# Value product with weight units taken in pairs and first pieces on two DMA queues, residual load and index-key norm moved

## The chip, the cores and the metric

The kernel runs on one core of a Trainium2 chip. The metric is the device time of one execution in microseconds (us), taken as the median of several runs; less is better. One further execution was profiled, and all rows below come from that one.

## What is computed

One decoder block on a sequence of 256 positions of 1024 channels, in float32. Cut to the parts that this change touches:

```
proj = h @ w_in[i]
u, v, q, k, vv, q_idx, k_idx, w_idx, g_a, g_b = jnp.split(proj, SPLIT_POINTS, axis=-1)
...
k_idx = layer_norm(k_idx, ln_kidx_g[i], ln_kidx_b[i])
b_out = dsa_attention(q, k, vv, q_idx, k_idx, w_idx)
mix = sigmoid(g_a) * (a_out @ w_branch_a[i]) + sigmoid(g_b) * (b_out @ w_branch_b[i])
y = mix @ w_o[i]
h = layer_norm(ALPHA * h + y, ln1_g[i], ln1_b[i])
...                                   # FFN with a causal convolution, second norm
```

`vv` is the value product, the first of the kernel. The indexer scores of `dsa_attention` need the normalised `k_idx`. The residual `h` in `ALPHA * h + y` is the input `x`.

## The kernel before

**Weights.** All weights stream from DRAM once as units of 128 x 2048 float32 (1 MB), in the order of use, through `prefetch` (line 83) and `take`. A unit lands in a raw buffer (pool `rawp`, three buffers) by a DMA issued on SyncE (SP). `split` (line 74) then writes a rounded copy `hi` on ScalarE (ACT, line 77) and the rest `lo = raw - hi` on VectorE (DVE, line 78); both are kept in pools of five. A product is the sum of three: x_hi w_hi, x_lo w_hi, x_hi w_lo. `take()` asks for units up to four ahead of the one in use. A raw buffer is free again when its `lo` is written.

**The start.** Eight warm-up matmuls run on constants (line 121). The input, transposed and cut into eight x blocks of 128 channels (`xt_sb`, 128 KB each), is split into `xh` and `xl`. `load_unit` (line 130) brings unit 0 in four pieces of 256 KB with one x block after each, unit 1 in two, then x blocks 4 to 7 in one load, then unit 2 in two; unit 3 comes whole through `prefetch`.

**The value product** (line 239) has four accumulators of 128 x 512 in PSUM. Units 0 and 1 hold the two column halves for x blocks 0 to 3, units 2 and 3 those for blocks 4 to 7. The loop takes one unit at a time: four x blocks, each three parts for two row tiles, six matmuls of 512 columns a block, 96 in all. Copies to SBUF (line 243) follow each of the last two units. Index queries (`qi`), the small index-key product (`kwb`), queries, keys and gates follow.

**Index keys.** `kidx_norm` (normalisation of the index keys, on PE, DVE and ACT) is hooked into the first half of the first query unit, `kidx_transpose` into the first half of the third; `indexer_head` runs for heads 0 to 3 behind the third query unit and for 4 to 7 behind the fourth.

**The residual.** After the output gates (line 464) the residual `hres` is loaded into slot `ga`, which the gates use until then (line 468, GpSimd's queue, POOL). `o_half(t, hf)` multiplies by `w_o` for row tile t and column half hf, then adds the residual (line 488) and takes statistics (489). `ln1_apply` normalises (lines 415, 416), and `h_transpose` transposes on PE (line 503). The order is o_half(0,0), o_half(0,1), ln1_apply(0), o_half(1,0), h_transpose(0, ...), o_half(1,1).

**What sets the order.** Each engine runs its instructions in the order in which a scheduler at build time has put them, close to the order of the code. SP waits in order, too: a DMA that must wait for a free buffer, or for one of eight completion semaphores that DMAs use in turn (`DMAHW0` to `DMAHW7`), holds back those behind it.

Of the kernel before, what the change touches and what calls it, by code (L numbers as in the profile page):

```python
# [9 lines left out]
F32 = mybir.dt.float32  # L10
# [5 lines left out]
P = 128  # L16
L = 256
D = 1024
# [22 lines left out]
def kernel(  # L41
# [88 lines left out]
    def load_unit(pieces, pre=None):  # L130
        i = state["next"]
        state["next"] += 1
        raw = rawp.tile([P, UN], F32, tag="raw", name=f"raw{i}")
        hi = hip.tile([P, UN], F32R, tag="hi", name=f"hi{i}")
        lo = lop.tile([P, UN], F32R, tag="lo", name=f"lo{i}")
        n = UN // pieces
        for c in range(pieces):
            cs = slice(c * n, (c + 1) * n)
            nc.sync.dma_start(out=raw[:, cs], in_=wst[i][:, cs])
            if pre:  # L140
                pre(c)
                with tc.issue_after(prev.ins) if c else nullcontext():
                    nc.vector.tensor_copy(xh[:, c:c + 1], xt_sb[:, c:c + 1])
                nc.vector.tensor_tensor(out=xl[:, c:c + 1], in0=xt_sb[:, c:c + 1], in1=xh[:, c:c + 1].bitcast(F32),
                                        op=ALU.subtract)
            m = max(1, n // 512)
            for d in range(m):
                ds_ = slice(c * n + d * n // m, c * n + (d + 1) * n // m)
                prev = split(hi[:, ds_], lo[:, ds_], raw[:, ds_])[1]
        units[i] = (hi, lo)  # L150

    load_unit(4, lambda c: load_x(c, c + 1))
    load_unit(2)
    load_x(4, 8)
    split(xh[:, 4:8], xl[:, 4:8], xt_sb[:, 4:8])
    load_unit(2)
# [20 lines left out]
    def fm_chunks(hi, lo, m2, bank, hook=None):  # L177
        wh = hi.rearrange("p (k n) -> p k n", n=256)
        wl = lo.rearrange("p (k n) -> p k n", n=256)
        for c in range(2):  # L180
            cs = slice(c * P, (c + 1) * P)
            fm_tile(bank[:, c], lambda k: wh[:, k, cs], lambda k: wl[:, k, cs], m2, hook if c == 0 else None)

    def fm_unit(name, m2, hook=None):
        hi, lo = take()
        bank = bankA([P, 2, 2, L], name)
        fm_chunks(hi, lo, m2, bank, hook)
        return bank
# [43 lines left out]
    for kh in range(2):  # L232
        for hf in range(2):
            hi, lo = take()
            for k in range(4):
                for n, (a, b) in enumerate(((xh, hi), (xl, hi), (xh, lo))):
                    kk = 4 * kh + k
                    for t in range(2):
                        nc.tensor.matmul(vbanks[2 * t + hf], a[:, kk, t * P:(t + 1) * P], b[:, k * 512:k * 512 + 512],  # L239
                                         start=kk == 0 and n == 0, stop=kk == KC - 1 and n == 2)  # L240
            if kh == 1:
                for t in range(2):
                    nc.scalar.copy(vv[:, t, hf * 512:(hf + 1) * 512], vbanks[2 * t + hf])
# [56 lines left out]

    def causal_fill(dst, fill):
# [155 lines left out]

    m2 = slot("x2", [P, 2, 8, L], F32R, name="m2")
# [8 lines left out]
    hres = slot("ga", [P, 2, D], name="hres")  # L467
    nc.gpsimd.dma_start(out=hres, in_=x.rearrange("(t p) d -> p t d", p=P))
    l1p = slot("k", [P, 2, D], name="l1p")
    ln1_g = load_par(l1p[:, 0], "ln1_g")  # L470
    ln1_b = load_par(l1p[:, 1], "ln1_b")
    cv_sb = const.tile([P, 4, 44], F32, name="cv_sb")
    nc.sync.dma_start(out=cv_sb, in_=cv)
# [256 lines left out]
```

## Time and profile before

| | us |
|---|---|
| median of 3 runs | 462.25 |
| lowest and highest | 462.13 and 463.82 |
| the profiled execution, whole | 462.86 |
| span of its instructions | 461.1 |
| PE busy | 450.6 (98%) |
| DVE busy | 356.7 (77%) |
| ACT busy | 260.8 (57%) |

The span runs from the first instruction of the program to the last. PE's busy time is modelled: a matmul that has to wait in the middle of a stream counts as busy, so starts of neighbouring matmuls say more than busy shares. PEld is the loading of PE's stationary operand, beside the matmuls. An entry in brackets at a row's end is the idle time of the engine before it, and what ended it.

### The profile page before, as it was taken

The page shows a single profiled execution, that of the slowest core. Times are in us where ns is not written, and L with a number is a line of the kernel's source. Part 1 is how long each engine was busy: PE and PEld are TensorE (multiplying, and loading weights), DVE is VectorE, ACT ScalarE, POOL GpSimd, SP SyncE. Part 2 cuts the span into 40 slices and gives each one's busy share as a digit, 9 for nine tenths or more (in the row PEclk, how much of TensorE's full clock was granted, in tenths as well). Part 3 has the DMA queues.
Part 4 walks back from the last instruction along what each step waited for, and adds up shares of the span by engine and source line. Part 5 has one row for each costly group of instructions (what it writes and reads, how often), then busy time and mean ns, then how long its engine had stood idle before and what let it go on. Part 6 is the DMA issues. An engine that isn't in the chain of part 4 may idle for free.

```text
span 461.1 us, 6365 instructions
## 1 busy us (share of the span) xinstructions
PE 450.6 (98%) x2470; PEld 388.3 (84%) x2470; DVE 356.7 (77%) x582; ACT 260.8 (57%) x381; POOL 9.0 (2%) x19
## 2 busy tenths in 40 slices
PE   8999999999999999999999899999999999999993
PEld 5788898888888888888888699888888888888883
DVE  3869869977787559588785769999878778777746
ACT  3678744466656447645454228987656655656500
POOL 0000001020000100001000000000000000000000
PEclk9999999999999999999999999999999999999998
DMA  7979763555433644737746026846755554551002
GB/s 221 388 271 343 266 239 136 183 183 183 182 124 151 224 171 156 248 117 252 298 179 244 31 92 247 302 153 212 273 182 183 183 188 178 207 200 50 1 0 91
DMA packets 14989, 86.83 MB, mean 188 GB/s; under 512 B 1648, under 2 KB 2928, under 8 KB 5744
## 3 DMA queue, kind: packets, MB, share of 16 engines
q1 hardware_dynamic: 13536, 81.98, 49.1%
q0 software_dynamic: 1136, 4.19, 2.7%
q8 instruction: 19, 0.31, 0.3%
q10 hardware_dynamic: 288, 0.26, 0.2%
q14 instruction: 10, 0.08, 0.0%
HBM read 85.39 MB, written 1.05 MB: 187 GB/s over the span
## 4 chain that ended last, share of the span: by engine, by line
PE 78%; issue 8%; DVE 6%; DMA 5%; ACT 1%; SPq 1%; POOL 0%; DVEq 0%; POOLq 0%; ACTq 0%
PE up L173 16%; PE up L175 8%; PE g L173 6%; PE dn L109 4%; PE dn L110 4%; PE dn L111 4%; PE g L175 3%; PE k L173 3%; PE u L173 3%; DVE lo L78 3%; PE vv L239 3%; PE wb L173 2%; PE u L175 2%; PE k L175 2%; PE v L109 2%
## 5 line engine op out<-in xcount | busy, mean ns | idle before, releaser
L78 DVE TENSOR_TENSOR lo<-raw,hi 128x1024 fp32r<-128x1024 f32 (+1 forms) x158 | 180.0, 1169 | 51.6 <-ACT hi L77 50.7
L77 ACT CAST hi<-raw 128x1024 fp32r<-128x1024 f32 (+1 forms) x158 | 152.7, 1006 | 94.5 <-PE up L173 16.8
L173 PE MATMUL up<-h,hi 128*128 128x512 f32 x320 | 80.3, 392 | 0.0
L173 PEld LDWEIGHTS up<-h,hi 128*128 128x128 f32 x320 | 57.9, 189 | 10.6
L175 PEld LDWEIGHTS up<-h,lo 128*128 128x128 f32 x320 | 43.7, 190 | 3.1
L175 PE MATMUL up<-h,lo 128*128 128x256 f32 x320 | 44.6, 282 | 0.0
L531 ACT ACTIVATE y<-upf,cv_sb 128x256 f32<-128x256 f32 x40 | 21.9, 594 | 20.3 <-DVE upf L194 20.3
L173 PE MATMUL g<-x,hi 128*128 128x512 f32 x128 | 32.9, 399 | 0.0
L173 PEld LDWEIGHTS g<-x,hi 128*128 128x128 f32 x128 | 23.0, 189 | 4.3 <-DVE kT L194 0.2
L532 DVE SCALAR_TENSOR_TENSOR y<-upf,cv_sb,y 128x255 f32<-128x255 f32 x40 | 18.7, 479 | 9.4 <-ACT y L531 9.4
L239 PE MATMUL vv<-hi,x 128*128 128x512 f32 x64 | 19.3, 424 | 0.7 <-ACT hi L77 0.6
L534 DVE SCALAR_TENSOR_TENSOR y<-upf,cv_sb,y 128x254 f32<-128x254 f32 x40 | 18.8, 480 | 1.0
L175 PEld LDWEIGHTS g<-x,lo 128*128 128x128 f32 x128 | 17.4, 190 | 1.3
L175 PE MATMUL g<-x,lo 128*128 128x256 f32 x128 | 17.8, 282 | 0.0
L239 PEld LDWEIGHTS vv<-hi,x 128*128 128x128 f32 x64 | 12.8, 205 | 5.1 <-ACT hi L77 1.5
L173 PE MATMUL wb<-b,hi 128*128 128x512 f32 x64 | 16.3, 396 | 0.0
L173 PE MATMUL k<-x,hi 128*128 128x512 f32 x64 | 16.2, 395 | 0.0
L173 PE MATMUL q<-x,hi 128*128 128x512 f32 x64 | 16.2, 394 | 0.0
L173 PE MATMUL u<-x,hi 128*128 128x512 f32 x64 | 16.1, 393 | 0.0
L173 PE MATMUL wa<-a,hi 128*128 128x512 f32 x64 | 16.0, 392 | 0.0
L194 DVE TENSOR_TENSOR upf<-up,upf 128x512 f32<-128x512 f32 x20 | 13.7, 683 | 0.5 <-ACT upf L193 0.5
L173 PEld LDWEIGHTS k<-x,hi 128*128 128x128 f32 x64 | 11.5, 189 | 2.2 <-DVE kT L194 0.2
(222 smaller groups left out, 819.9 us busy)
## 6 DMA issues: line engine op xcount, KB each, us to landing
raw<-in_wst_dram SPq DMA_DIRECT2D x72, 1024.0 KB, 4.8
raw<-in_wst_dram SPq DMA_DIRECT2D x4, 512.0 KB, 8.7
raw<-in_wst_dram SPq DMA_DIRECT2D x4, 256.0 KB, 4.9
a2a<-in_par_dram POOLq DMA_DIRECT2D x2, 512.0 KB, 5.9
l1p<-in_par_dram POOLq DMA_DIRECT2D x2, 512.0 KB, 6.8
hres<-in_x_dram POOLq DMA_DIRECT2D x1, 1024.0 KB, 7.3
xt_sb<-in_xt_dram SPq DMA_DIRECT2D x4, 128.0 KB, 4.8
xt_sb<-in_xt_dram SPq DMA_DIRECT2D x1, 512.0 KB, 8.9
```

What stands on the lines that cost most here:

```text
L77: a = nc.scalar.copy(hi, src)
L78: return a, nc.vector.tensor_tensor(out=lo, in0=src, in1=hi.bitcast(F32), op=ALU.subtract)
L109: nc.tensor.matmul(ps, ah, bh, start=start, stop=False)
L110: nc.tensor.matmul(ps, ah, bl, start=False, stop=False)
L111: nc.tensor.matmul(ps, al, bh, start=False, stop=stop)
L173: nc.tensor.matmul(ps, wh(k), m2[:, :, k, :], start=k == 0, stop=False)
L175: nc.tensor.matmul(ps[:, 0, :], wl(k), m2[:, 0, k, :], start=False, stop=k == KC - 1)
L194: nc.vector.tensor_tensor(out=dst, in0=bank[:, :, 0, :], in1=dst, op=ALU.add)
L239: nc.tensor.matmul(vbanks[2 * t + hf], a[:, kk, t * P:(t + 1) * P], b[:, k * 512:k * 512 + 512], start=kk == 0 and n == 0, stop=kk == KC - ...
L531: nc.scalar.activation(y[:, c, :], b[:, c, :], AF.Identity, scale=cv_sb[:, 2, ch:ch + 1], bias=cv_sb[:, 3, ch:ch + 1])
L532: nc.vector.scalar_tensor_tensor(y[:, c, 1:], b[:, c, :L - 1], cv_sb[:, 1, ch:ch + 1], y[:, c, 1:], op0=ALU.mult, op1=ALU.add)
L534: nc.vector.scalar_tensor_tensor(y[:, c, 2:], b[:, c, :L - 2], cv_sb[:, 0, ch:ch + 1], y[:, c, 2:], op0=ALU.mult, op1=ALU.add)
```

## The change

The first two units, and then units 2 and 3, are opened as a pair (`open_pair`). In each of x blocks 0 to 3 both units of the pair get two DMA pieces of 128 x 256 (128 KB). For the first block one piece of each unit is issued on ACT's queue, the others on SP's. For the first block half of unit 0's `hi` is made on DVE instead of ACT. x blocks 4 to 7 come in two loads with halves of units 2 and 3. The matmul loop takes each x block through both units. The four copies of the result come at the end. `kidx_norm` is hooked into the second half of its query unit, heads 0 to 3 into the first half of the fourth. The residual goes to slot `q`, which held the gated values `vn` (read last by `spatial`), and its load is written ahead of the `wa` product; the first FFN tile takes slot `ga` in return.

```diff
+    def split_x(a, b, after=None):
+        with tc.issue_after(after.ins) if after else nullcontext():
+            c = nc.vector.tensor_copy(xh[:, a:b], xt_sb[:, a:b])
+        return c, nc.vector.tensor_tensor(out=xl[:, a:b], in0=xt_sb[:, a:b], in1=xh[:, a:b].bitcast(F32), op=ALU.subtract)
...
+    first_two = open_pair()
+    u0, u1 = first_two
+    load_w(u0, 0, 256)
+    load_w(u0, 256, 512, nc.scalar)
+    load_x(0, 1)
+    load_w(u1, 0, 256, nc.scalar)
+    load_w(u1, 256, 512)
+    prev = None
+    for c in range(4):
+        cs = slice(c * 512, (c + 1) * 512)
+        if c:
+            load_x(c, c + 1)
+            for u in first_two:
+                load_w(u, c * 512, c * 512 + 256)
+                load_w(u, c * 512 + 256, c * 512 + 512)
+        cast, xs = split_x(c, c + 1, prev)
+        if c:
+            for u in first_two:
+                nc.scalar.copy(u[2][:, cs], u[1][:, cs])
+            after = xs
+        else:
+            nc.scalar.copy(u0[2][:, 0:256], u0[1][:, 0:256])
+            with tc.issue_after(cast.ins):
+                w = nc.vector.tensor_copy(u0[2][:, 256:512], u0[1][:, 256:512])
...
+            nc.scalar.copy(u1[2][:, cs], u1[1][:, cs])
+            after = xs
+        with tc.issue_after(after.ins):
+            for u in first_two:
+                prev = low(u, c * 512, c * 512 + 512)
+    pair = open_pair()
+    for c in range(2):
+        load_x(4 + 2 * c, 6 + 2 * c)
+        for u in pair:
+            load_w(u, c * 1024, c * 1024 + 1024)
...
     for kh in range(2):
-        for hf in range(2):
-            hi, lo = take()
-            for k in range(4):
-                for n, (a, b) in enumerate(((xh, hi), (xl, hi), (xh, lo))):
-                    kk = 4 * kh + k
+        pair = [take() for _ in range(2)]
+        for k in range(4):
+            kk = 4 * kh + k
+            for n, (a, part) in enumerate(((xh, 0), (xl, 0), (xh, 1))):
+                for hf in range(2):
                     for t in range(2):
-                        nc.tensor.matmul(vbanks[2 * t + hf], a[:, kk, t * P:(t + 1) * P], b[:, k * 512:k * 512 + 512],
+                        nc.tensor.matmul(vbanks[2 * hf + t], a[:, kk, t * P:(t + 1) * P], pair[hf][part][:, k * 512:k * 512 + 512],
                                          start=kk == 0 and n == 0, stop=kk == KC - 1 and n == 2)
...
     for u in range(4):
-        b = fm_unit(f"q{u}", x2, {0: kidx_norm, 2: kidx_transpose}.get(u))
+        b = fm_unit(f"q{u}", x2, *{0: (kidx_norm, 1), 2: (kidx_transpose, 0), 3: (lambda: heads(0, 4), 0)}.get(u, ()))
         fold(b, qT[:, 2 * u:2 * u + 2, :])
-        if u > 1:
-            for h in range(4 * u - 8, 4 * u - 4):
-                indexer_head(h)
+    heads(4, 8)
...
+    hres = slot("q", [P, 2, D], name="hres")
+    nc.gpsimd.dma_start(out=hres, in_=x.rearrange("(t p) d -> p t d", p=P))
...
-    hres = slot("ga", [P, 2, D], name="hres")
-    nc.gpsimd.dma_start(out=hres, in_=x.rearrange("(t p) d -> p t d", p=P))
...
-    f_slots = ["q", ("fa", 0), ("fa", 1), ("fx", 0), ("fx", 1), "k"]
+    f_slots = ["ga", ("fa", 0), ("fa", 1), ("fx", 0), ("fx", 1), "k"]
```

The order of instructions as built shows three places. First SP's DMAs where unit 3 (`raw3`) is loaded, the kernel before, with what each waits for (`DVE` is the release of a raw buffer):

```order
L139 DMA raw1_120<-in_wst_dram 128x1024 [waits DMAHW1_49]
L128 DMA xt_sb_91<-in_xt_dram 128x1024 [waits DMAHW2_49]
L139 DMA raw2_136<-in_wst_dram 128x1024 [waits DMAHW3_49]
L139 DMA raw2_136<-in_wst_dram 128x1024 [waits DMAHW4_49]
L90 DMA raw3_163<-in_wst_dram 128x2048 [waits DMAHW6_49,DMAHW5_49,DVE_49]
```

The same place on SP in the changed kernel:

```order
L148 DMA raw1_96<-in_wst_dram 128x256 [waits DMAHW3_49]
L128 DMA xt_sb_91<-in_xt_dram 128x512 [waits DMAHW4_49]
L148 DMA raw2_144<-in_wst_dram 128x1024 [waits DMAHW5_49]
L148 DMA raw3_147<-in_wst_dram 128x1024 [waits DMAHW1_49,DMAHW6_49,DMAHW0_49,DVE_49]
L128 DMA xt_sb_91<-in_xt_dram 128x512 [waits DMAHW7_49]
L148 DMA raw2_144<-in_wst_dram 128x1024
L148 DMA raw3_147<-in_wst_dram 128x1024
L90 DMA raw4_190<-in_wst_dram 128x2048 [waits DMAHW3_49,DMAHW2_49,DVE_49]
```

The first half of unit 3, which waits for a free raw buffer, now stands ahead of x blocks 6 and 7 and of the second halves of units 2 and 3. Second, the first rows on DVE, before (`x2` holds `xh` and `xl`):

```order
L143 CAST x2_92<-xt_sb_91 128x256 [waits DMAHW1_49]
L144 TENSOR_TENSOR x2_92<-xt_sb_91,x2_92 128x256 [waits DVE_49]
L78 TENSOR_TENSOR lo0_95<-raw0_93,hi0_94 128x512 [waits DMAHW0_49,Activation_49]
L143 CAST x2_92<-xt_sb_91 128x256 [waits DMAHW3_49]
L78 TENSOR_TENSOR lo0_95<-raw0_93,hi0_94 128x512 [waits DMAHW2_49,Activation_49]
```

And after:

```order
L132 CAST x2_92<-xt_sb_91 128x256 [waits DMAHW3_49]
L177 CAST hi0_94<-raw0_93 128x256 [waits DMAHW0_49]
L133 TENSOR_TENSOR x2_92<-xt_sb_91,x2_92 128x256 [waits DVE_49]
L152 TENSOR_TENSOR lo0_95<-raw0_93,hi0_94 128x512 [waits DMAHW1_49,DVE_49,Activation_49]
L152 TENSOR_TENSOR lo1_98<-raw1_96,hi1_97 128x512 [waits DMAHW4_49,DMAHW2_49,Activation_49]
L132 CAST x2_92<-xt_sb_91 128x256 [waits DMAHW5_49]
```

A cast of half the first weight piece has moved to DVE, behind the cast of the x block. Third, on POOL, one piece of the difference:

```order
 L115 DMA a2a<-in_par_dram 128x1024 x2
+L500 DMA hres<-in_x_dram 128x2x1024
 L115 DMA ln_g<-in_par_dram 128x1024
 L115 DMA ln_b<-in_par_dram 128x1024
 L115 DMA l1p<-in_par_dram 128x1024 x2
-L468 DMA hres<-in_x_dram 128x2x1024
```

The residual's load has moved ahead of four parameter loads.

## Rows read from the trace of the kernel before

**Rows 1.** The page, part 1: busy us, share of the span, instructions.

```profile
span 461.1 us, 6365 instructions
...
PE 450.6 (98%) x2470; PEld 388.3 (84%) x2470; DVE 356.7 (77%) x582; ACT 260.8 (57%) x381; POOL 9.0 (2%) x19
```

**Rows 2.** Waits of PE: engine line waited for: us in total, times, longest.

```profile
PE hT L503 <- DVE hres L416: 1.5, 1, 1.5
...
PE kT2ps L284 <- DVE a2a L279: 0.2, 1, 0.2
```

**Rows 3.** Timeline of PE, start: start us, us, engine line op out<-in, count [idle before].

```profile
0.85 3.57 PE L121 MATMUL wps<-const-bfloat16-1.0 128*128 128x512 bf16 x8 [0.85 <-PEq L719]
...
5.00 2.04 PE L239 MATMUL vv<-hi,x 128*128 128x512 f32 x4 [0.58 <-ACT hi L77]
...
14.70 1.07 PE L239 MATMUL vv<-hi,x 128*128 128x512 f32 x4
...
28.30 1.07 PE L239 MATMUL vv<-hi,x 128*128 128x512 f32 x4
...
29.66 1.98 PE L173 MATMUL qi<-x,hi 128*128 128x512 f32 x8
```

**Rows 4.** Windows of line 239 alone: PE busy (matmuls), PEld, clock, DMA share, GB/s.

```profile
5.00:9.40 4.40, 4.40 (x10) 3.44 (x11) 1.00 0.90 213
```

**Rows 5.** Timeline of SP's DMA issues, start.

```profile
0.81 0.37 SPq L139 DMA_DIRECT2D raw<-in_wst_dram  x1
...
4.07 0.43 SPq L128 DMA_DIRECT2D xt_sb<-in_xt_dram  x1
...
11.93 0.33 SPq L90 DMA_DIRECT2D raw<-in_wst_dram  x1
```

**Rows 6.** Timeline of ACT and DVE, start.

```profile
4.27 0.62 ACT L77 CAST hi<-raw 128x512 fp32r<-128x512 f32 x1 [2.19 <-DMA raw<-in_wst_dram]
...
4.56 0.29 DVE L143 CAST x<-xt_sb 128x256 fp32r<-128x256 f32 x1 [4.56 <-DMA xt_sb<-in_xt_dram]
...
5.23 0.68 DVE L78 TENSOR_TENSOR lo<-raw,hi 128x512 fp32r<-128x512 f32 x1
...
11.02 0.29 DVE L143 CAST x<-xt_sb 128x256 fp32r<-128x256 f32 x1 [1.01 <-DMA xt_sb<-in_xt_dram]
```

**Rows 7.** Windows: PE, PEld, DVE, ACT, POOL busy, clock, DMA share, GB/s.

```profile
5.00:9.40 4.40, 4.40 (x10) 3.44 (x11) 2.95 (x7) 1.24 (x2) 0.00 (x0) 1.00 0.90 213
...
13.00:19.00 6.00, 6.00 (x28) 4.94 (x27) 5.57 (x9) 4.89 (x8) 0.00 (x0) 1.00 1.04 419
```

**Rows 8.** DMA issues by tile: count, KB each, median us to landing.

```profile
xt_sb<-in_xt_dram SPq DMA_DIRECT2D x4, 128.0 KB, 4.8
...
wk_sb<-in_wk_dram SPq DMA_DIRECT2D x1, 288.0 KB, 3.3
```

**Rows 9.** Timeline of POOL, DVE and PE where the residual is added and transposed.

```profile
249.17 0.70 POOL L468 DMA_DIRECT2D hres<-in_x_dram  x1 [32.61 <-DVE gb L464]
...
254.76 0.39 PE L109 MATMUL o<-hi,m 128*128 128x512 f32 x1
...
256.55 0.69 DVE L488 SCALAR_TENSOR_TENSOR hres<-hres,o 128x512 f32<-128x512 f32 x1 [6.28 <-DMA hres<-in_x_dram]
...
257.89 0.67 DVE L488 SCALAR_TENSOR_TENSOR hres<-hres,o 128x512 f32<-128x512 f32 x1
...
259.98 0.39 PE L111 MATMUL o<-hi,m 128*128 128x512 f32 x1
...
261.89 1.32 PE L503 MATMUL hT<-ident,hres 128*128 128x128 f32 x8 [1.53 <-DVE hres L416]
```

**Rows 10.** Timeline of POOL behind the last spatial product.

```profile
210.56 0.53 POOL L115 DMA_DIRECT2D ln_g<-in_par_dram  x1 [56.79 <-PE sp L433]
```

**Rows 11.** Timeline of PE at the second key transpose.

```profile
57.60 0.33 PE L284 MATMUL kT2ps<-ident,a2a 128*128 128x128 f32 x1 [0.15 <-DVE a2a L279]
```

**Rows 12.** Timeline of DVE, a pair of weight subtractions beside the index-key chain.

```profile
47.67 2.35 DVE L78 TENSOR_TENSOR lo<-raw,hi 128x1024 fp32r<-128x1024 f32 x2
```

More of the change, by code (lines that the diff above doesn't have):

```diff
@@ L128, in load_x @@
         nc.sync.dma_start(out=xt_sb[:, a:b], in_=xt[:, a:b])
[L130 to L156, printed above, removed]
+    def split_x(a, b, after=None):
+        with tc.issue_after(after.ins) if after else nullcontext():
+            c = nc.vector.tensor_copy(xh[:, a:b], xt_sb[:, a:b])
+        return c, nc.vector.tensor_tensor(out=xl[:, a:b], in0=xt_sb[:, a:b], in1=xh[:, a:b].bitcast(F32), op=ALU.subtract)
+    def open_pair():
+        pair = []
+        for i in (state["next"], state["next"] + 1):
+            raw = rawp.tile([P, UN], F32, tag="raw", name=f"raw{i}")
+            hi = hip.tile([P, UN], F32R, tag="hi", name=f"hi{i}")
+            lo = lop.tile([P, UN], F32R, tag="lo", name=f"lo{i}")
+            units[i] = (hi, lo)
+            pair.append((i, raw, hi, lo))
+        state["next"] += 2
+        return pair
@@ new lines, in load_w, with low @@
+    def load_w(unit, a, b, eng=None):
+        i, raw, _, _ = unit
+        (eng or nc.sync).dma_start(out=raw[:, a:b], in_=wst[i][:, a:b])
+    def low(unit, a, b):
+        _, raw, hi, lo = unit
+        return nc.vector.tensor_tensor(out=lo[:, a:b], in0=raw[:, a:b], in1=hi[:, a:b].bitcast(F32), op=ALU.subtract)
+    first_two = open_pair()
[5 more added lines that the diff above has]
+    load_w(u1, 256, 512)
@@ new lines @@
+    prev = None
[15 more added lines that the diff above has]
+                w = nc.vector.tensor_copy(u0[2][:, 256:512], u0[1][:, 256:512])
+            tc.add_manual_dep(xs.ins, w.ins.name, mybir.DependencyInfo(mybir.DependencyClass.NoSync, mybir.DependencyReason.DATA), reason="order")
+            nc.scalar.copy(u1[2][:, cs], u1[1][:, cs])
[3 more added lines that the diff above has]
+                prev = low(u, c * 512, c * 512 + 512)
@@ new lines @@
+    pair = open_pair()
[3 more added lines that the diff above has]
+            load_w(u, c * 1024, c * 1024 + 1024)
+        _, xs = split_x(4 + 2 * c, 6 + 2 * c, prev)
+        for d in range(2):
+            for u in pair:
+                ds_ = slice(c * 1024 + d * 512, c * 1024 + d * 512 + 512)
+                nc.scalar.copy(u[2][:, ds_], u[1][:, ds_])
+                with tc.issue_after(xs.ins):
+                    prev = low(u, ds_.start, ds_.stop)
@@ L299, in indexer_head, with heads @@
                                                op0=ALU.mult, op1=ALU.add)
+    def heads(a, b):
+        for h in range(a, b):
+            indexer_head(h)
     def causal_fill(dst, fill):
@@ L456 @@
             spatial(u + 2)
+    hres = slot("q", [P, 2, D], name="hres")
+    nc.gpsimd.dma_start(out=hres, in_=x.rearrange("(t p) d -> p t d", p=P))
+    l1p = slot("k", [P, 2, D], name="l1p")
+    ln1_g = load_par(l1p[:, 0], "ln1_g")
+    ln1_b = load_par(l1p[:, 1], "ln1_b")
+    cv_sb = const.tile([P, 4, 44], F32, name="cv_sb")
+    nc.sync.dma_start(out=cv_sb, in_=cv)
     m2 = slot("x2", [P, 2, 8, L], F32R, name="m2")
@@ L465 @@
         split(mh[:, us, :], ml[:, us, :], gb[:, us, :], 0.5)
-    hres = slot("ga", [P, 2, D], name="hres")
-    nc.gpsimd.dma_start(out=hres, in_=x.rearrange("(t p) d -> p t d", p=P))
[L469 to L473, printed above, removed]
     ous = [take(0) for _ in range(4)]
```

14 lines of the change are left out of this document (7 added, 7 removed).

## Prediction

> **What bounds the kernel now.** I read the busy shares first, then who waits for whom on TensorE (PE), then the timelines of the two places that those waits name, and last the DMA rates of the first 20 us. The span is 461.1 us and PE is busy in 98% of it [rows 1], so time can only come from the few places where PE waits or runs slowly. The waits are few: 1.5 us at the transposes of the normalised residual, and 0.2 us at the transpose of the index keys [rows 2]. A third place hides in the busy time: the value product at the start, whose matmuls last longer because they stretch over waits or run at the lower clock. Ten of its matmuls of 512 columns take 4.40 us, 0.44 each [rows 4], the pace of the 1.2 GHz level, as did the eight warm-up matmuls in 3.57 us; from 14.70 to 28.30, ten rounds of six take 13.60 us, 0.227 each [rows 3], the pace of the 2.4 GHz level. (The clock column prints 1.00 in both; the spacing tells the level.) The stage ends when the next product starts, at 29.66 [rows 3]. With the ten slow ones done at 9.40, the other 86 need 86 x 0.227 = 19.5 us and would end at 28.9. So 0.76 us went to waits for data, between 9.40 and 14.70. That is all that a better supply can give once PE runs.
>
> **Part 1, the residual load.** Before, the 1 MB load of the residual stands last on POOL, behind the release of its slot by the last gate sum. It is issued at 249.17, and the first operation that needs it starts at 256.55, after 6.28 us of idle VectorE (DVE) [rows 9]. From the second of those operations (257.89) to the first transpose (261.89) is a chain of 4.00 us: statistics, root, two passes. PE had finished the third output product's last matmul, begun at 259.98, and could have started the transposes 0.227 later, at 260.21. It starts them at 261.89: 1.68 us lost. After, the load takes the slot of the gated values, free once the spatial products have read them. The POOL load that waits for exactly that PE work today goes out at 210.56 [rows 10]; so the residual lands some 30 us before its use. The chain then starts when the second output product ends, about 254.9 (the third starts at 254.76 [rows 9]), and ends at 258.9, 1.3 us before PE asks. I take the whole 1.68. What pays: POOL spends 0.70 us on the issue, with four parameter loads behind it that are used tens of us later; 1 MB of traffic moves from 249 to 211, into a stretch where PE waits for nothing [rows 2] and weights are taken four units ahead. Both at nothing; if the cover failed, 1 MB at the 419 GB/s of large pieces [rows 7] is 2.5 us, against four units of 24 matmuls or their like, 5.4 us each. The swap of the slot for the first FFN tile costs nothing, as both slots are free by 249.
>
> **Part 2, the value product in pairs.** The work stays 96 matmuls and 5 MB. What changes is what PE needs when. Before, one unit goes through four x blocks, six matmuls a block; now two units share a block, twelve matmuls, so a block of 640 KB is asked for every 12 x 0.227 = 2.72 us instead of 384 KB every 1.36. Four terms:
>
> *Start.* Before, the first matmul (5.00) follows the cast of the first x block on DVE (4.56, 0.29 long [rows 6]) by 0.15; the weights' cast on ScalarE (ACT) is done by then. Now DVE does two casts of that size in a row, since half of the first weight piece is cast there: 4.56 + 0.29 + 0.29 + 0.15 = 5.29. This supposes that x lands when it does today: it is the second issue on SP as before. The row for what stands beside it is the rate of the first stage, 213 GB/s between 5.0 and 9.4 [rows 7]: one more 128 KB piece ahead of x (the second unit's, from ACT) is 0.6 us, so up to 5.9; and x could land up to 0.3 earlier, since the piece ahead of it on SP is halved. I take 5.29. The Trainium skill (DMA: Bandwidth & Descriptors, "Issuing engines are not separate DMA queues") says that DMAs issued from several engines share the same DMA engines, and that a second issuer saves only the time of issuing. By it the second unit's piece delays x as if it stood on SP, the start is 5.9, and the forecast would be 460.5.
>
> *Slow stretch.* I keep the rise of the clock at 9.40. From 5.29 that is 9.3 matmuls, and 86.7 are left: 19.65 us, end at 29.05 without waits. Against 29.66 that gains 0.61; from a start at 5.00 it would be 0.77, from 5.9 it is 0.3 (a later start costs half its length, since it is paid in slow matmuls).
>
> *Supply of the first four blocks.* These are 20 pieces of 128 KB, 18 of them on SP. SP issues one every 0.466 us (eight issues from 0.81 to 4.07 [rows 5]), so the last goes out at 0.81 + 17 x 0.466 = 8.7 and lands 4.8 later, by the row of the 128 KB pieces [rows 8]: 13.5. Block 3 begins at 9.40 + 26.7 x 0.227 = 15.45 and wants that piece, cast in 0.62, some 0.5 later: 1.8 us in hand. The slow end: the fourth x block of today, issued at 4.07, landed at 11.02 [rows 5, 6] with 1.57 MB ahead of it, 174 GB/s from 2.0 on; at that pace the 2.62 MB end at 17.1, and PE waits 1.8 us.
>
> *The fourth unit.* There are three raw buffers. The first half of the fourth unit can be issued only when the first unit is split to the end, and the order of SP shows that wait, with the rest of the x blocks and five weight issues behind it. Before, this wait ended at 11.93 [rows 5], and PE came to that unit at 24.2. Now PE wants it right at block 4: 15.45 + 2.72 + 3 x 0.227 = 18.85. The first unit's last piece lands at 12.6, cast 0.62, subtracted 0.68 [rows 6]: issue at 13.9, landing 4.8 later, cast 0.62: 19.3, 0.5 late. With the 3.3 us of the 288 KB load [rows 8] it is 17.8, in time. I take 0.25. At the slow end of the supply it is 2.3 late, on top of the 1.8.
>
> Sum of part 2: 0.61 - 0.25 = 0.36 us gained; bounds +0.77 and 0.61 - 4.1 = -3.5. I choose near the upper end, because the pieces of 4 KB rows and more run at 419 GB/s [rows 7] and the slow pace ends with the first small pieces. The four copies of the result now come together behind the last matmul instead of two and two; their banks are wanted again over 10 us later: nothing.
>
> **Part 3, index keys and heads.** The same instructions move. PE waits for the second key transpose at 57.60, 0.15 us [rows 11]. In DVE's new order the subtraction that stood ahead of the last key additions (half of a pair that takes 2.35 [rows 12]) gives way to a shorter fold, but the whole chain of normalisation hangs on ACT and DVE, and PE now comes earlier by what part 2 gains. Ends: the wait and its refill gone, +0.3; one pair of subtractions late, -2.35. The total work ahead of it is the same, so I take 0. Four heads move into the last query product: same matmuls, no wait there before, nothing.
>
> **Sum.** The profiled execution took 462.86: the 461.1 of the span and 1.76 around it. Less 1.68 + 0.36 + 0 = 2.04 gives 460.8. The median of the runs lies 0.61 under the profiled one, so 462.25 - 2.04 = 460.2.
>
> **Rivals.** *Supply clears it all:* x lands a little earlier, no wait at the fourth unit, the key wait goes: 1.68 + 0.77 + 0.3 = 2.75, 459.5. For it: only 0.5 us is missing at the fourth unit by a pessimistic landing time. Against: the two casts in a row on DVE.
>
> *The clock rises later.* Today it rises after PE ran from 5.00 to 9.40 without a break, behind a break of 0.58 [rows 3, 4]. A later start, or a gap in the first two blocks while the second unit's pieces land, can move the rise. Each us costs 0.5 us (0.44 against 0.227 a matmul). The Trainium skill (TensorE: Matmul & The Clock Gate, Part 1) says that the throttled state is the default and that activity releases it; the two paces in the rows agree. A rise 2 us later takes 1.0: 461.2. Against: twelve slow matmuls are 5.3 us of work on the first block alone, so the next block has time to land.
>
> *Slower: the small pieces.* If 1 KB rows keep the 174 GB/s through all 2.62 MB, block 3 and the fourth unit wait 4.1 us in all, and the time is 462.25 - 1.68 + 3.5 = 464.1. It passes the old time from a loss of 1.7 us in part 2, that is, from 2.3 us of waits: where the early pieces average under some 197 GB/s, so that the last lands at 15.3 and the fourth unit is 2.3 late. For it: 213 GB/s between 5.0 and 9.4 [rows 7], with rows of 1 and 2 KB. Against: the early rate is no worse for having more issues if they stay ahead.
>
> **How the numbers follow.** Forecast 460.2 with its neighbours (459.8 to 460.8) 0.50; supply clears it 0.24; late clock (460.8 to 461.8) 0.18; small pieces 0.08. The range 459.1 to 461.8 leaves out the small pieces and the ends of the others. A measurement of this kernel tells about 0.5% from no change: under 459.94 or over 464.56. Faster by that: nearly all of the second case and about a third of the first, 0.40. Slower by that: half of the last, 0.04. Within: 0.56.
>
> **What would show it.** Part 1 is right if VectorE no longer idles for the residual and the first transposes follow the third product without idle time; wrong if PE still waits there for the second pass. Part 2 is right if the first product of the next stage starts at 29.2 to 29.4, the first value matmul at about 5.3, and PE shows at most a short wait where the fourth unit comes in; wrong if the start is at 5.8 or later, or if the ten or so slow matmuls become fifteen. Part 3 is right if the waits at the key transposes stay under 0.5 us. The forecast falls if a new wait of over 1 us stands in the first 60 us, or if PE waits anywhere from 205 to 250.

## The result and the profile after

The changed kernel takes 467.99 us (median of four runs, 466.96 to 469.0), the kernel before beside it on the same chip 463.03. The ratio is 1.011, with a 95% interval of 1.008 to 1.0139: slower by 5 us, where 2 us faster was forecast. The profiled execution took 466.96, with a span of 465.2 against the 461.1 of [rows 1], so the profile shows 4.1 us of the loss; it is the shortest of the four runs.

The waits of PE first (engine, line, what was waited for: us in total, times, longest):

```profile
PE kwp L305 <- DVE a2a L299: 2.0, 1, 2.0
PE vv L278 <- ACT hi L172: 1.7, 2, 0.8
PE vv L278 <- DVE hi L177: 1.6, 1, 1.6
PE vv L278 <- ACT hi L193: 1.4, 1, 1.4
```

Against [rows 2], the wait of 1.5 us at the residual's transposes (`hT`) is gone, and 5.1 us of waits stand in the value product and at the index keys' first transposes (`kwp`; the 1.6 at the start replaces the 0.58 of [rows 3]). The timeline of PE shows where they are:

```profile
5.72 2.08 PE L278 MATMUL vv<-hi,x 128*128 128x512 f32 x8 [1.61 <-DVE hi L177]
...
12.73 1.66 PE L278 MATMUL vv<-hi,x 128*128 128x512 f32 x6 [0.85 <-ACT hi L172]
...
16.13 2.35 PE L278 MATMUL vv<-hi,x 128*128 128x512 f32 x8 [0.81 <-ACT hi L172]
...
21.45 1.43 PE L278 MATMUL vv<-hi,x 128*128 128x512 f32 x5 [1.38 <-ACT hi L193]
...
32.16 1.98 PE L212 MATMUL qi<-x,hi 128*128 128x512 f32 x8
...
53.63 0.32 PE L305 MATMUL kwp<-ident,a2a 72*128 72x72 f32 x2 [2.02 <-DVE a2a L299]
...
54.07 2.91 PE L212 MATMUL q<-x,hi 128*128 128x512 f32 x8
56.78 1.78 PE L214 MATMUL q<-x,lo 128*128 128x256 f32 x8
58.40 1.99 PE L212 MATMUL q<-x,hi 128*128 128x512 f32 x8
60.23 1.12 PE L214 MATMUL q<-x,lo 128*128 128x256 f32 x8
61.18 1.55 PE L212 MATMUL q<-x,hi 128*128 128x512 f32 x6
...
76.29 2.00 PE L212 MATMUL k<-x,hi 128*128 128x512 f32 x8
```

Follow the starts of the stages. The index queries (`qi`) begin at 32.16 instead of 29.66 [rows 3]: 2.50 us late. The first key unit begins at 76.29; in the trace before it began so:

```profile
70.45 2.00 PE L173 MATMUL k<-x,hi 128*128 128x512 f32 x8
```

That is 5.84 late, so 3.34 more went between the two. Of these, 2.02 are the wait at `kwp`. About 1.55 are the 16 matmuls behind it: from 54.07 to 58.40 they take 4.33 us, and the next 16, from 58.40 to 61.18, 2.78. The windows there (us, PE busy, PEld, DVE, ACT, POOL, granted clock, DMA share, GB/s) tell why:

```profile
53.60:54.80 1.20, 1.17 (x8) 1.07 (x9) 1.20 (x2) 0.53 (x2) 0.00 (x0) 1.00 0.35 75
54.80:58.30 3.50, 3.50 (x14) 3.02 (x13) 3.32 (x8) 3.17 (x4) 0.00 (x0) 0.51 1.02 389
58.30:62.00 3.70, 3.70 (x22) 3.25 (x22) 2.47 (x10) 2.17 (x6) 0.00 (x0) 1.00 0.64 217
```

The granted clock is 0.51 in the middle stretch, the 1.2 GHz level, and 1.00 on both sides; PE had stood idle for 2.02 us until 53.63, and the fall came some 1.2 us behind that.

The supply of weights is behind this, as the experiments below show. SP's issues in the value stage, and the first issue behind them:

```profile
10.17 1.30 SPq L128 DMA_DIRECT2D xt_sb<-in_xt_dram  x1
11.52 5.64 SPq L148 DMA_DIRECT2D raw<-in_wst_dram  x2
17.21 0.43 SPq L128 DMA_DIRECT2D xt_sb<-in_xt_dram  x1
```

The two issues in the middle are the first halves of units 2 and 3. An issue takes some 0.45, so SP stood for about 4.7 us ahead of the second, until 16.7: unit 3 had to wait for unit 0's raw buffer, and everything else waited behind it. The buffer came free so late because unit 0's last piece came late. ACT could start on it only at 15.46, and DVE's subtraction, the first of the two below, ended near 16.8:

```profile
15.46 1.31 ACT L172 CAST hi<-raw 128x512 fp32r<-128x512 f32 x2 [2.78 <-DMA raw<-in_wst_dram]
16.11 1.38 DVE L152 TENSOR_TENSOR lo<-raw,hi 128x512 fp32r<-128x512 f32 x2 [0.67 <-ACT hi L172]
```

The same windows of both traces (columns as above), first after, then before:

```profile
10.00:12.00 2.00, 1.88 (x9) 1.23 (x7) 0.64 (x1) 0.00 (x0) 0.00 (x0) 1.00 0.72 114
12.00:14.00 2.00, 1.27 (x6) 1.05 (x7) 0.69 (x1) 0.62 (x1) 0.00 (x0) 1.00 0.95 288
14.00:16.00 2.00, 1.32 (x6) 0.75 (x4) 0.72 (x2) 0.54 (x1) 0.00 (x0) 1.00 0.85 281
16.00:18.00 2.00, 1.87 (x7) 1.30 (x8) 1.85 (x4) 0.70 (x2) 0.00 (x0) 1.00 0.13 43
```

```profile
10.00:12.00 2.00, 1.97 (x9) 1.11 (x7) 0.99 (x4) 0.23 (x1) 0.00 (x0) 1.00 1.03 414
12.00:14.00 2.00, 1.86 (x8) 1.42 (x8) 1.32 (x3) 1.60 (x3) 0.00 (x0) 1.00 1.01 414
14.00:16.00 2.00, 2.00 (x10) 1.67 (x9) 1.57 (x4) 1.74 (x3) 0.00 (x0) 1.00 1.04 428
16.00:18.00 2.00, 2.00 (x10) 1.65 (x10) 2.00 (x3) 1.77 (x4) 0.00 (x0) 1.00 1.01 410
```

In these 8 us 1.45 MB came instead of 3.33. The missing 1.9 MB are 4.6 us at 410 GB/s. There are two holes, one from 10 to 12 (114 GB/s while the DMA engines are busy 0.72 of the time) and one from 16 to 18 (43 GB/s, the engines busy 0.13 of it). In the first hole only SP's queue moved bytes (244 packets, 0.23 MB), so no other stream took the engines' time.

How this reaches the index keys stands in the timelines of ACT and DVE:

```profile
45.88 2.00 ACT L77 CAST hi<-raw 128x1024 fp32r<-128x1024 f32 x2 [1.79 <-DMA raw<-in_wst_dram]
```

```profile
50.79 2.36 DVE L78 TENSOR_TENSOR lo<-raw,hi 128x1024 fp32r<-128x1024 f32 x2
53.07 0.41 DVE L299 TENSOR_TENSOR a2a<-kwb,a2a 72x256 f32<-72x256 f32 x1
```

A unit's weights land late: ACT casts them at 45.88, after 1.79 us without work, and all that stands behind on ACT and DVE is late with them. On DVE a pair of subtractions, that of the next unit, stands ahead of the index keys' sum (line 299), and PE waits for that sum. Before, the sum ran at 47.33, ahead of such a pair [rows 12]:

```profile
47.33 0.42 DVE L260 TENSOR_TENSOR a2a<-kwb,a2a 72x256 f32<-72x256 f32 x1
```

The last stage went as the prediction said. The transposes start behind the last product without idle time:

```profile
265.72 0.39 PE L111 MATMUL o<-hi,m 128*128 128x512 f32 x1
265.95 1.03 PE L544 MATMUL hT<-ident,hres 128*128 128x128 f32 x8
266.74 0.48 PE L109 MATMUL o<-hi,m 128*128 128x512 f32 x1
```

### The profile page after: what moved, and what is told of

It reads as the page before. It is cut to its first block, busy times and chain, and to the rows that moved or that the text cites. A ratio compares the mean times of both kernels' runs of the same rounds, so it can differ in the third digit from the quotient of the medians.

```text
span 465.2 us, 6391 instructions
## 1 busy us (share of the span) xinstructions
PE 450.1 (97%) x2470; PEld 387.9 (83%) x2470; DVE 358.7 (77%) x586; ACT 260.3 (56%) x380; POOL 8.1 (2%) x19
## 3 DMA queue, kind: packets, MB, share of 16 engines
HBM read 85.39 MB, written 1.05 MB: 186 GB/s over the span
## 4 chain that ended last, share of the span: by engine, by line
PE 87%; DMA 7%; DVE 3%; SPq 1%; ACT 1%; issue 0%; DVEq 0%; ACTq 0%
PE up L212 16%; PE up L214 8%; DMA raw<-in_wst_dram 7%; PE g L212 6%; PE dn L110 4%; PE dn L109 4%; PE dn L111 4%; PE g L214 3%; PE k L212 3%; PE wb L212 3%; PE wa L212 3%; PE u L212 3%; PE q L212 3%; PE wa L214 2%; PE wb L214 2%; PE u L214 2%
## 5 line engine op out<-in xcount | busy, mean ns | idle before, releaser
L78 DVE TENSOR_TENSOR lo<-raw,hi 128x1024 fp32r<-128x1024 f32 x142 | 169.8, 1224 | 50.6 <-ACT hi L77 49.6
L77 ACT CAST hi<-raw 128x1024 fp32r<-128x1024 f32 x142 | 143.5, 1049 | 90.2 <-PE up L212 17.2
L278 PE MATMUL vv<-hi,x 128*128 128x512 f32 x64 | 17.2, 401 | 4.7 <-ACT hi L172 1.7
L278 PEld LDWEIGHTS vv<-hi,x 128*128 128x128 f32 x64 | 11.5, 188 | 9.6 <-ACT hi L172 2.9
L212 PE MATMUL q<-x,hi 128*128 128x512 f32 x64 | 17.2, 411 | 0.0
L152 DVE TENSOR_TENSOR lo<-raw,hi 128x512 fp32r<-128x512 f32 x16 | 10.6, 689 | 6.5 <-ACT hi L193 3.4
```

The source lines that it names most:

```text
L77: a = nc.scalar.copy(hi, src)
L78: return a, nc.vector.tensor_tensor(out=lo, in0=src, in1=hi.bitcast(F32), op=ALU.subtract)
L212: nc.tensor.matmul(ps, wh(k), m2[:, :, k, :], start=k == 0, stop=False)
L278: nc.tensor.matmul(vbanks[2 * hf + t], a[:, kk, t * P:(t + 1) * P], pair[hf][part][:, k * 512:k * 512 + 512], start=kk == 0 and n == 0, st ...
```

## The experiments

Each is a kernel of its own, timed beside the kernel before (its median lay between 462.55 and 463.03 in every group). I write "own place" for an own SBUF slot of the fourth unit's raw weights.

### Each part alone

**e1_residual**: the kernel before with the residual's load moved, and with it the parameter loads written behind it, as in the change.

```diff
-    hres = slot("ga", [P, 2, D], name="hres")          # behind the wa product
+    hres = slot("q", [P, 2, D], name="hres")           # ahead of it
...
-    f_slots = ["q", ("fa", 0), ...
+    f_slots = ["ga", ("fa", 0), ...
```

> The kernel before with the residual's slot and load moved alone. Theory (three separate effects): this part gains what the two traces show between the gate product and the first FFN product, about 1.9 us, so 461.1 where the kernel before has 463.0, a ratio of 0.996; no idle time of TensorE ahead of the transposes of the normalised residual. Rival (the gain shows only because the kernel after comes late there): within 0.3 us of the kernel before.

Measured: 461.06, ratio 0.9952 (0.9933 to 0.997), span 459.2. PE no longer waits at `hT`, and the product behind the transposes begins at 261.03 instead of 262.96, 1.93 us earlier (first this run, then the kernel before):

```profile
261.03 0.48 PE L109 MATMUL o<-hi,m 128*128 128x512 f32 x1
```

```profile
262.96 0.48 PE L109 MATMUL o<-hi,m 128*128 128x512 f32 x1
```

Part 1 stands.

**e2_keys**: the kernel before with the hooks of the index keys and heads moved.

```diff
-        b = fm_unit(f"q{u}", x2, {0: kidx_norm, 2: kidx_transpose}.get(u))
+        b = fm_unit(f"q{u}", x2, *{0: (kidx_norm, 1), 2: (kidx_transpose, 0), 3: (lambda: heads(0, 4), 0)}.get(u, ()))
...
+    heads(4, 8)
```

> The kernel before with the index-key norm and the heads moved alone. Theory (the 2.0 us wait ahead of the index-key transposes and the lower clock behind it come from the late supply of weights out of the value stage): within 0.5 us of the kernel before, 463.0, and no wait at those transposes. Rival (they come from the moved norm itself): 2.5 to 4 us slower, 466 to 467, with a wait of about 2 us at the first index-key transposes.

Measured: 462.75, ratio 0.999 (0.9971 to 1.0008). By itself part 3 costs nothing: the wait at `kwp` in the changed kernel is not the fault of the hooks.

**e3_pairs**: the kernel before with the value product in pairs and its new loads.

```diff
-    load_unit(4, lambda c: load_x(c, c + 1))
+    first_two = open_pair()
...
-        for hf in range(2):
-            hi, lo = take()
+        pair = [take() for _ in range(2)]
```

> The kernel before with the value product in pairs and its small first pieces alone, norm and residual as before. Theory (the value stage costs 2.5 us itself and its late supply another 3.5 at the index keys): 468.5 to 470, the first query-index product starting near 32.2, and a wait of 2 us or a little more at the first index-key transposes. Rival (the wait comes from the moved norm): 465 to 466, and no wait at the index keys.

Measured: 469.57 (468.41 to 473.08), ratio 1.014 (1.0087 to 1.0193). The whole loss is in part 2, and it shows the same two places: the index queries start at 30.96 (32.2 was expected), and PE waits for the index keys although their hooks are the old ones:

```profile
53.76 0.32 PE L305 MATMUL kwp<-ident,a2a 72*128 72x72 f32 x2 [3.36 <-DVE a2a L299]
```

Here PE came to that point 1.2 us earlier than in the changed kernel and left it 0.13 later. So an earlier arrival of PE did not help: what it waits for came no earlier.

**e4_fold_first**: in the changed kernel, the loading and splitting of one unit put behind the index keys' sum, so that its subtractions no longer stand ahead of that sum on DVE.

```diff
-        b = fold(fm_unit(f"qi{u}", x2), name=f"qif{u}")
+        b = fold(fm_unit(f"qi{u}", x2, ahead=AHEAD - u), name=f"qif{u}")
...
-    nc.vector.tensor_tensor(out=kwT[0:72, :], in0=kwb[:, 0], in1=kwT[0:72, :], op=ALU.add)
+    kwf = nc.vector.tensor_tensor(out=kwT[0:72, :], in0=kwb[:, 0], in1=kwT[0:72, :], op=ALU.add)
+    with tc.issue_after(kwf.ins):
+        prefetch(cur["i"] + AHEAD - 1)
```

> The kernel after with one weight unit's loading and splitting put behind the fold of the index keys on VectorE, so that this fold no longer stands behind a pair of weight subtractions. Theory (TensorE's 2.0 us wait there is this one pair in VectorE's order, and the drop of the clock behind it follows from the wait): wait under 0.3 us, no lower clock there, 3.4 us faster than the kernel after, about 464.5. Rival (the fold is late in any case, since its inputs are late): wait over 1 us and a time within 1 us of the kernel after, 467 to 468.

Measured: 467.11 (464.71 to 468.07). Only 0.9 us came back, which is within the spread of the runs. The wait stayed (2.72 us in this profile), and a second one appeared at the next transposes:

```profile
52.94 0.32 PE L307 MATMUL kwp<-ident,a2a 72*128 72x72 f32 x2 [2.72 <-DVE a2a L299]
...
63.13 0.33 PE L325 MATMUL kT2ps<-ident,a2a 128*128 128x128 f32 x1 [1.45 <-DVE a2a L320]
```

On ACT the unit ahead of that one waits 3.36 us for its raw weights, and ACT's copy of the key sum stands behind it:

```profile
47.45 2.00 ACT L77 CAST hi<-raw 128x1024 fp32r<-128x1024 f32 x2 [3.36 <-DMA raw<-in_wst_dram]
...
50.63 0.37 ACT L298 COPY a2a<-kwb 72x256 f32<-72x256 f32 x1
```

My theory of the order fell: with the weights late, the sum waited in the new order too.

### The supply: buffer or small pieces

**e5_256kb**, on the changed kernel:

```diff
-                load_w(u, c * 512, c * 512 + 256)
-                load_w(u, c * 512 + 256, c * 512 + 512)
+                load_w(u, c * 512, c * 512 + 512)
```

and likewise in the first block, all on SP.

> The changed kernel with the first two units in pieces of 256 KB instead of 128 KB, all on SP's queue; the pairs, the order of the matmuls and the rest stay. Buffer theory (the fourth unit waits for a raw buffer that the pair gives back late, and SP stands still with all weights behind it): SP is still held until about 16 to 17 us, the wait for the index keys stays, 466.5 to 468.5. Rival (the 128 KB pieces move too slowly): the first four blocks land earlier, the waits of 0.85 and 0.81 us go and the weights behind come earlier too, 463.5 to 465.5.

**e6_own_raw**, on the changed kernel:

```diff
+            if i == 3:
+                raw = slot("ga", [P, UN], name="raw3")
+            else:
+                raw = rawp.tile([P, UN], F32, tag="raw", name=f"raw{i}")
-            raw = rawp.tile([P, UN], F32, tag="raw", name=f"raw{i}")
```

> The changed kernel with a place of its own in SBUF for the raw weights of the fourth unit (the slot of the first gate tile, free then), so that its load waits for no buffer. Buffer theory: SP runs on at 11.5 us, the rate between 16 and 18 us is above 200 GB/s instead of 43, the 1.38 us before the fourth unit go, and with the supply 3 to 5 us earlier the wait for the index keys (2.0 us) and the half clock behind it (1.7 us) shrink: 462.5 to 465.5. Rival (small pieces): the pieces of blocks 2 and 3 land as late as now, and at best the 1.38 us before the fourth unit go, which the wait for the index keys then swallows: 466.5 to 468.

**e8_both**: both edits.

> Both edits: pieces of 256 KB on one queue and an own place for the fourth unit's raw weights. If buffer hold and small pieces each cost something, this is the fastest of the three, 461.0 to 463.0, near the old kernel less the 1.9 us of the residual. If it lies with the own place alone, within 0.5 us, only the buffer counts; if with the 256 KB alone, only the pieces. If it stays above 465, neither is the cause, and the order of the matmuls itself is (two units must be split before the second block).

Measured: 465.67 (462.44 to 466.77) with large pieces, 463.13 (0.998 to 1.0015 of before) with the own place, 460.92 (0.9946 to 0.9976) with both. From 467.99 that is 2.3, 4.9 and 7.1: the two causes add up within the spread of the runs, and the buffer is the larger. With both gone the kernel is as fast as with part 1 alone (461.06); a gain from the pairs doesn't show. The large pieces alone came out between the two cases set for them (463.5 to 465.5, and 466.5 to 468.5), as both count; in that profile SP was still held, but only until 13.4. The windows show the two holes close one by one; first the own place, then both edits:

```profile
10.00:12.00 2.00, 1.99 (x9) 1.31 (x7) 1.01 (x2) 0.44 (x1) 0.00 (x0) 1.00 0.88 124
...
16.00:18.00 2.00, 2.00 (x6) 1.56 (x5) 1.86 (x5) 0.76 (x3) 0.00 (x0) 0.51 0.90 288
```

```profile
10.00:12.00 2.00, 2.00 (x9) 1.61 (x9) 1.97 (x6) 1.26 (x3) 0.00 (x0) 1.00 1.05 380
...
16.00:18.00 2.00, 2.00 (x11) 1.65 (x10) 2.00 (x5) 1.15 (x2) 0.00 (x0) 1.00 1.03 381
```

With the own place the wait at `kwp` falls to 0.26 us, with both it is gone:

```profile
51.23 0.32 PE L308 MATMUL kwp<-ident,a2a 72*128 72x72 f32 x2 [0.26 <-DVE a2a L302]
```

With the own place the hooks, the pairs and the order on DVE up to the key sum are as in the changed kernel, and the weights come earlier. With both edits one thing more differs: the scheduler has put the key sum ahead of the two pairs of subtractions (it runs at 43.34), so that run by itself doesn't part supply and order; e6_own_raw does.

### Which small pieces

**e13_first_only**, own place, small pieces over two queues in the first block alone:

```diff
-                load_w(u, c * 512, c * 512 + 256)
-                load_w(u, c * 512 + 256, c * 512 + 512)
+                load_w(u, c * 512, c * 512 + 512)
```

> The kernel with the fourth unit's own raw place (463.13), with 128 KB pieces over two queues in the first x block only and 256 KB pieces in blocks 1 to 3. If the two queues and small pieces of the first block cost the early supply, it stays at 462.5 to 463.5; if the twelve small pieces of blocks 1 to 3 do, it goes to the 460.9 of the kernel with 256 KB throughout, 460.5 to 461.5.

**e14_one_queue**, own place, all small pieces on SP:

```diff
-    load_w(u0, 256, 512, nc.scalar)
+    load_w(u0, 256, 512)
...
-    load_w(u1, 0, 256, nc.scalar)
+    load_w(u1, 0, 256)
```

> The kernel with the fourth unit's own raw place (463.13), with all its 128 KB pieces on SP's queue and none on ACT's. If the second queue slows the early packets of the first, it is faster, 461 to 462.5; if only the number of pieces counts, it stays at 462.7 to 463.7, the first value matmul up to 0.9 us later for the two issues more on SP ahead of x.

**e12_2kb_rows**, own place, as many 128 KB pieces in blocks 1 to 3, but of 64 partitions with 2 KB rows (`rows` chooses the partitions):

```diff
...
-                load_w(u, c * 512, c * 512 + 256)
-                load_w(u, c * 512 + 256, c * 512 + 512)
+                load_w(u, c * 512, c * 512 + 512, rows=(0, 64))
+                load_w(u, c * 512, c * 512 + 512, rows=(64, 128))
```

> The kernel with the fourth unit's own raw place (463.13), and in blocks 1 to 3 the same number of 128 KB pieces, but each with 64 partitions of 2 KB rows instead of 128 of 1 KB. If the short rows are what slows the early stage, it goes to the time with 256 KB pieces, 460.8 to 461.8, and the rate from 8 to 12 us is above 300 GB/s instead of 204 and 124. Rival (the number of issues, 0.47 us each on SP, or the pieces' number): 462.7 to 463.7 and the rate stays.

Measured: 460.97, 462.4 and 463.26, against 463.13 for the own place alone. So by the medians 2.2 us are the price of the small pieces of blocks 1 to 3; for those of the first block no price shows against 256 KB throughout (460.92). The size is less sure than the direction, since the intervals against the kernel before (0.9953 to 0.9993 for e13_first_only, 0.998 to 1.0015 for the own place alone) meet at their ends. On one queue it is 0.7 faster, at the edge of the range for a cost of the second queue, but the intervals against the kernel before (0.9977 to 1.0015 here, 0.998 to 1.0015 there) overlap. The start differs clearly: the first value matmul ran at 4.89, where with two queues it ran at 5.57:

```profile
4.89 2.57 PE L281 MATMUL vv<-hi,x 128*128 128x512 f32 x8 [0.48 <-DVE hi L180]
```

A later start had been allowed for here, not an earlier one. The other profiles bear it out: it ran at 5.53 to 5.91 in all nine with two queues, and at 5.16 to 5.23 in the three with 256 KB pieces on one.

Longer rows at the same piece size changed nothing, and 143 GB/s from 10 to 12 us is hardly more than the 124 of the own place alone, so the length of a row is not the cause as it was put here. Whether it is the number of pieces in flight or that a piece then covers half the partitions, the runs don't part. Nor are small pieces slow at all times: in the changed kernel they moved at 341 GB/s from 4 to 6 us (750 packets) and at 114 from 10 to 12 (244 packets). Why the rate sinks in between stays open.

### The wait at the index keys and the clock behind it

**e9_kwp_later**, on the changed kernel:

```diff
-        b = fm_unit(f"q{u}", x2, *{0: (kidx_norm, 1), 2: (kidx_transpose, 0), 3: (lambda: heads(0, 4), 0)}.get(u, ()))
+        b = fm_unit(f"q{u}", x2, *{1: (kidx_norm, 0), 2: (kidx_transpose, 1), 3: (lambda: heads(0, 4), 1)}.get(u, ()))
```

> The changed kernel with the index keys' first transposes taken up half a query unit later (first half of the second unit), the second ones half a unit later (second half of the third), and the first four heads half a unit later. Theory (TensorE loses 2.0 us waiting there and 1.7 us in the slow clock behind that gap; the loads behind are in time): both go, 463.8 to 465.2. Rival (the whole supply is late, so a wait only moves on): a new wait of the same length stands at the second transposes or at a query unit, 466.5 to 469.

Measured: 467.08 (463.17 to 469.06), and in the profiled run the wait had moved with the hook:

```profile
55.43 0.32 PE L305 MATMUL kwp<-ident,a2a 72*128 72x72 f32 x2 [2.15 <-DVE a2a L299]
```

In that run the rival holds: with the supply late, a later place for its user met a later release. The ten runs do not all tell this. Four, with a granted clock of 0.996 or 0.997, took 463.17 to 465.18, about what the theory gave; the other six, the profiled one among them, had 0.991 to 0.994 and took 466.79 to 469.06. Whether the wait stood in the four is not on record.

**e11_busy_gap** and **e15_no_idle**, on the changed kernel, with 8 and with 18 matmuls on constants ahead of `kwp`:

```diff
+        wps2 = bankB([P, 512], "wps2")
+        for _ in range(8):            # 18 in e15_no_idle
+            nc.tensor.matmul(wps2, zero[:, 0:P], zero, start=True, stop=True)
         kwp = bankB([P, 2, 72], "kwp")
```

> The changed kernel with eight more matmuls on constants (128x512, 0.23 us each, 1.8 in all) right ahead of the index keys' first transposes, into a bank that nobody reads: they fill the wait of 2.0 us, and nothing else changes. Theory (the clock halves because PE stood idle there): the half clock behind it is gone, -1.7, 465.8 to 467.0. Rival (the clock falls for another reason, or the time is given back at the second key transposes, which come earlier): 467.3 or more.

> The changed kernel with eighteen matmuls on constants ahead of the index keys' first transposes, 4.1 us, enough to reach the time at which the subtraction behind the weights lets them go (53 to 55 us), so that TensorE does not stand idle there. Theory (idle TensorE makes the clock halve, and that is what parts the changed kernel's slow runs of 467 to 469 from its others): the clock stays at 1.00 to the end of the stage, median 465.0 to 467.0, no run over 468. Rival (the clock halves anyway, or the time is lost again at the second transposes): 467.3 or more.

Measured: 468.88 (466.11 to 471.52) and 467.46 (466.51 to 468.2); the theory allowed at most 467.0 for either. The eight did not fill the wait. They ran from 49.38 on, ahead of it, and 3.98 us of idle time followed; the clock fell inside that time:

```profile
51.10:53.00 1.90, 0.00 (x0) 0.00 (x0) 1.84 (x3) 1.78 (x2) 0.00 (x0) 1.00 0.57 121
53.00:55.00 2.00, 0.00 (x0) 0.00 (x0) 2.00 (x4) 1.75 (x2) 0.00 (x0) 0.54 1.02 430
55.00:59.90 4.90, 4.84 (x17) 4.29 (x18) 4.24 (x9) 2.52 (x4) 0.00 (x0) 0.50 0.87 306
```

The eighteen left 1.39 us idle, and the clock stayed at 1.00 throughout:

```profile
49.50 4.11 PE L305 MATMUL wps<-const-bfloat16-1.0 128*128 128x512 bf16 x18
55.01 0.32 PE L308 MATMUL kwp<-ident,a2a 72*128 72x72 f32 x2 [1.39 <-DVE a2a L299]
```

So the half clock goes with the idle time, as the theory had it, though not with every such time: the 2.72 us of e4_fold_first passed without it. The Trainium skill (TensorE: Matmul & The Clock Gate, Part 1) says that the throttled state is the default and activity releases it; these rows agree. But the median with eighteen is only 0.5 lower than that of the changed kernel: the key sum let PE go at 55.01, 1.4 us later than in the profile of the changed kernel. The price of the half clock is thus shown by the rows of one profile (1.55 us), not by the time of a kernel without it.

### Versions that keep the gain

**e7_res_keys** is the changed kernel with the old value product, and **e10_keys_back** has pairs with both supply edits and the residual's move, but the old hooks (the edits of e1 and e2, and of e1, e3 and e8).

> The changed kernel with the old value product (one unit after another, old pieces): the moves of the residual and of the index keys alone. If the two add up (-1.9 and -0.2 us measured alone), 460.7 to 461.2. Rival: the earlier end of the residual stage or the key moves hinder each other, 461.5 or more.

> Pairs with 256 KB pieces and the fourth unit's own raw place, the residual moved, but the index keys and heads in their old places. If the key moves cost what the profile shows at the second key transposes (0.56 us of waits), 460.2 to 460.7. Rival: with PE 0.85 us earlier the old places wait as much or more at the keys, since ACT and DVE set that chain, 460.9 to 461.5.

Measured: 460.46 (ratio 0.9954, 0.9942 to 0.9966) and 460.94 (0.996, 0.9948 to 0.9972). With e1_residual (461.06), e8_both (460.92) and e13_first_only (460.97) they lie within 0.6 us of each other, all faster than both kernels, by 0.3 to 0.5% against the one before; which of them is best the runs don't tell. (e7_res_keys was expected at 460.7 to 461.2 and came 0.24 under it.) Two of the five have no pairs, so once the supply is mended the pairs cost nothing, but no gain of theirs shows either. In e10_keys_back they bring the index queries to 28.91, 0.75 ahead of [rows 3], but 0.5 us go at the second key transposes, and the first key unit begins at 70.29, only 0.16 ahead of the kernel before. The hooks are not what causes those waits, since both places of the hooks have them (0.6 us in e8_both), as the rival of its expectation had it.

## Why the prediction was wrong

**Bound.** Right as far as it went: PE is the bound, and the waits named are where time could come from. What it left out is that the supply of weights had slack of its own, which part 2 then spent.

**Part 1** was right: 1.68 forecast, 1.93 measured alone. Inside the changed kernel the stretch from the first key unit to the product behind the transposes takes 190.45 us instead of 192.51, 2.06 less.

**Part 2, the start.** 5.29 was forecast, 5.72 came, inside the bound of 5.9. The input block was cast at 5.08 instead of 4.56. The step that failed is the sentence that x lands when it does today. The Trainium skill's rule, as the prediction cites it there, gave 5.9 and was the better guess; e14_one_queue agrees with it, as the start came at 4.89 once all pieces stood on one queue. That the pieces on ACT's queue hold x up is the likely reading; the packets themselves were not followed.

**Part 2, the slow stretch.** The rise was kept at 9.40. In the profiled run the first eight matmuls already took 2.08 us, the pace of the high level, so nothing was slow, and that gave back what ten slow matmuls cost before, 2.1 us. This was luck, not the change: in the profile of e9_kwp_later, whose start is the same, they took 3.51. The stage still ended at 32.16 rather than 29.05: of its 26.44 us, 96 x 0.227 = 21.8 are work at the high level, 3.0 are waits from 11.9 on, and the remaining 1.6 are matmuls that stretched over waits.

**Part 2, the supply.** The last piece of block 3 was to land at 13.5; the first cast of that block could start only at 15.46, between that and the slow bound of 17.1. Two blocks waited, 1.66 us in all. The term was sized with 4.8 us from issue to landing for each piece [rows 8] and SP's pace. The pieces on SP did land after 3.6 us in the median, but the last two, issued at 9.2 and 9.7, took 6.5, and the rate sank to 114 GB/s as they piled up. The bound was there, and I chose the wrong end of it: the 419 GB/s of [rows 7] belong to large pieces, and the argument that more issues make the early rate no worse did not hold.

**Part 2, the fourth unit.** 0.25 us was taken, 1.38 came. Unit 0's buffer came free near 16.7, not 13.9, as its last piece landed near 15.4, not 12.6 (before, that wait ended at 11.93 [rows 5], when PE was far from unit 3). This is the step whose omission decided the sign: the text names the rest of the x blocks and the weights as queued behind the waiting issue, and then prices only PE's wait for unit 3. The 4.7 us that SP stood put every later weight behind, and the price fell due some 35 us later. By e6_own_raw the hold costs 4.9 us, of which only 1.4 stand at unit 3; the term for the bytes that do not flow meanwhile was left at nothing.

**Part 3.** Taken at 0 with a lower bound of -2.35. Alone it is 0 (e2_keys). In the changed kernel 2.02 us of wait and 1.55 of half clock stand there, beyond the bound, caused by part 2: e3_pairs has the wait and the half clock with the hooks in their old places.

**Rivals.** "The small pieces" had the right sign and half the mechanism, at a chance of 0.08 and with 464.1, since it ended at the value product. "The clock rises later" did not happen in the profiled run. No rival followed SP's hold beyond the stage.

## What to carry to other kernels

When a change makes two streams advance together, ask when the first buffer of the pair comes back: both are now held to the end, and the queue that waits for one holds back all that is queued behind it. Price such a hold by the bytes that don't flow meanwhile, and look for the bill at the place where the prefetch's slack runs out, which may lie two stages on. A wait that stays when its user is moved, as in the profiles of e4 and e9, points at the supply: here reordering did not mend it, and a buffer did.

## What the runs showed of the hardware

- PE's clock fell to half behind idle times of 1.89 us (e6_own_raw), 2.02 (the changed kernel), 2.15 (e9_kwp_later), 3.36 (e3_pairs) and 3.98 (e11_busy_gap), and not behind 2.13 (e5_256kb, at `kT2ps`) and 2.72 (e4_fold_first). So a gap near 2 us can cost 1.5 us on top of itself (1.55 in the changed kernel), and in these runs its length alone did not tell whether it would.
- The rise at the start varies from run to run with the same code ahead of it: the first eight value matmuls took 2.08 us in the changed kernel's profile and 3.51 in that of e9_kwp_later, whose start is the same.
- Many small pieces in flight moved at a low rate: from 10 to 12 us 114 GB/s at a DMA share of 0.72 (changed kernel), against 380 at 1.05 once the same blocks came in 256 KB pieces on one queue (e8_both). In the same changed kernel they had moved at 341 from 4 to 6 us, so it is not their size alone; the cause is open. Nor does the rate from 10 to 12 alone set the time: with small pieces in the first block only it was 199 (e13_first_only), at the same time as e8_both. A second queue did not bring the first block earlier, but later (5.57 in e6_own_raw against 4.89 in e14_one_queue).
